# Which engine forms the low parts of seven-product weight forms, and when x's fourth form is made

## The chip, the cores and the metric

The kernel runs on one core of one Trainium2 chip. The metric is the device time of one execution in microseconds (us), the median over several runs. A core has TensorE (PE: matmuls; PEld is its weight load), VectorE (DVE), ScalarE (ACT), GpSimd (POOL) and SyncE (SP), each with an instruction queue of its own that it works off in order, and 16 DMA engines that all queues share. An instruction that has to wait holds up everything behind it in its queue. Here SP issues the loads of weights, and GpSimd issues DMAs that add.

## The reference

Two layers on x of 512 tokens by 1024 features, in float32. Each layer is an FFN, a mixer, a second FFN and a gated input embedding, each followed by a LayerNorm of `ALPHA * x + sublayer(x)`:

```python
def swiglu_ffn(x, w_gu, w_d):
    g, u = jnp.split(x @ w_gu, 2, axis=-1)
    return (jax.nn.silu(g) * u) @ w_d
...
for i in range(DEPTH):
    x = layer_norm(DN_ALPHA * x + 0.5 * swiglu_ffn(x, ffn1_wgu[i], ffn1_wd[i]), ln_g[i, 0], ln_b[i, 0])
    ... mixer: mlstm_mixer in layer 0, gmlp_mixer in layer 1
    x = layer_norm(DN_ALPHA * x + 0.5 * swiglu_ffn(x, ffn2_wgu[i], ffn2_wd[i]), ln_g[i, 2], ln_b[i, 2])
    ... gated embedding
```

The hidden width of the FFN is 2816, which is 22 blocks of 128. There are four FFNs; the change touches nothing else.

## The kernel before, in words

**High and low parts.** TensorE multiplies float32 in a reduced form (`F32R`). So each operand is cut into a high part, ScalarE's rounded copy, and a low part, the operand less its high part, and a product is three matmuls: high by high, x's low by the weight's high, x's high by the weight's low (`mm3`, L351 to L355). The low part is made in one of two ways:

```python
self.nc.vector.tensor_sub(lo[:, s], src[:, s], hi[:, s].bitcast(F32))       # on VectorE: L251, or later L257
...
self.nc.scalar.activation(lo[:, s], src[:, s], AF.Copy, scale=-1.0)         # by DMA: ScalarE, L248,
self.nc.gpsimd.dma_start(lo[:, s], src[:, s], accum_op=OP.add)              # then GpSimd's adding DMA, L249
```

**Chunks.** `ffn` works through the 22 hidden blocks in six chunks of 2, 4, 4, 4, 4 and 4. In chunks 0 to 3 gate and up columns of a block are plain products of x (tile `fps`, L1145 to L1149). In chunks 4 and 5 a pair of blocks (gate g and up u, two raw weight tiles of 1 MB) is made with seven products in place of eight, in the manner of Strassen and Winograd: x is cut into quarters (two halves of the features by two halves of the tokens), the raw weights too, and sums of quarters are multiplied. This document calls the four pairs of an FFN A and B (chunk 4), C and D (chunk 5), and their products A0 to A6 and so on. Each goes into tile `ups`.

**Weight forms.** `up_forms` makes the seven forms of a pair in the raw tiles themselves: 0 (`a11`) and 1 (`a12`) are gate quarters as loaded; 2 (`s2`) is two VectorE instructions (L141, L142) that write over gate quarter 0; 3 (`s1`) is the up sum left there; 4 (`s3`) is two more (L149, L150) that write over gate quarter 1 and over gate quarter 0, that is, over form 2; 5 (`s4`) is what stands in gate quarter 1; 6 (`a22`) is an up quarter. Form 4 can only be made when the parts of forms 1 and 2 are taken (`self.after`). `UP_BY_DMA` lists the forms whose low part is made by DMA; the rest are made on VectorE, and in chunks 4 and 5 (`W.apart`) that subtraction is put off: it is issued at the next `W.lows()`, and the form counts as made from then on (L257, function `done`). A form by DMA counts as made at once, when its DMA is issued.

**Down products.** The down projection of chunk c - 1 runs in chunk c, also with seven products (`Group`, tile `gps`, weights `wquarter`), one after each odd step. Each adds into x's residual on VectorE (L727). Its weight forms always have their low parts on VectorE.

**The order of a step.** In chunks 4 and 5, `up_products` writes out one step s per up product: the product; the residual add of the last down product (L727); on the seventh product the gating (L1064, and a split in chunk 5); the copy of the product's bank out of PSUM (ScalarE, L1045) or an add onto it (VectorE, L1048, L1050); the put-off low parts; on some steps of chunk 4 an entry of `formed.last`; `W.release()`, which hands the product's weight buffer on and so cuts the form four products ahead (ScalarE's high part, L242); Silu; `W.form_ahead(3)`, which makes the sums of the next three forms if they may be made; on odd steps the down product and the cutting of the next form of h (L905, L908). A product r needs bank 0 free for r = 2, 4 and 6, bank 3 for r = 5.

**Loads.** There are three raw buffers. `done` counts down the uses of a raw tile and issues the next load on SP as soon as a tile has none left, that is, after forms 4 and 5 of a gate tile and 3 and 6 of an up tile. On the device the load waits for whoever reads the tile last.

**x's forms.** `UpForms` makes four sums of x's quarters, once per FFN. `steps` is a list of small functions: in chunk 3 two are run per block index i from `FORM_AT` on (L1161), and what is left at the end of that chunk. `last` maps a step of chunk 4 to a function: step 0 the low part of t2 and both parts of t3 (L994 and, over the quarter of x itself, L358 and L359), step 2 the sum `x21` (tile `x_d`, L964), step 3 `t4` (L1002, and copies on ScalarE, L1003), step 4 `t4_low` (L1008, tile `t_f`). Product 2 uses t2, 3 uses t1, 4 uses t3, 6 uses t4.

Of the kernel before, what the change touches and what calls it, by code (L numbers as in the profile page):

```python
# [10 lines left out]
F32 = mybir.dt.float32  # L11
F32R = mybir.dt.float32r
AF = mybir.ActivationFunctionType
# [29 lines left out]
W_BUFS = 4  # L43
EXTRA = 2
PLE_EXTRA = 3
UP_BY_DMA = (1, 2, 4)


class Weights:
# [77 lines left out]
    def up_forms(self, g, u):  # L127
# [34 lines left out]
        self.after.update({s2: (a11,), s3: (a12, s2)})  # L162
        self.by_dma.update(made[r][1] for r in UP_BY_DMA)
        return [("main", js, make) for js, make in made]
# [158 lines left out]
def hybrid_trunk(ctx: ExitStack, tc, x, p, ln_g, ln_b, ffn1_wgu, ffn1_wd, ffn2_wgu, ffn2_wd,  # L323
# [25 lines left out]
    vec, sca, pool = nc.vector, nc.scalar, nc.gpsimd  # L349
# [7 lines left out]
    def split(hi, lo, src):  # L357
        sca.activation(hi, src, AF.Copy)  # L358
        vec.tensor_sub(lo, src, hi.bitcast(F32))  # L359
# [75 lines left out]
    FFN_CHUNKS = [2, 4, 4, 4, 4, 4]  # L435
    LAST = len(FFN_CHUNKS) - 1
    UP_FROM = 4
    FORM_AT = 3
    turn_p = []

    def ffn_weights(wgu, wd, name, ple=False):
# [231 lines left out]
    class Norm:  # L673


        def __init__(self, layer, k, out=None):
            self.out, self.st, self.rs = out, {}, {}
            self.deferred = out is None and k != 2
            self.at = (layer * 4 + k) * KB
            gb = act.tile([P, 2, D], F32, name="gb", tag="gb")  # L680
            self.g_bc, self.b_bc = gb[:, 0], gb[:, 1]
            o = (layer * 4 + k) * D
            sca.dma_start(self.g_bc, row_ap(ln_g, o, D))
            sca.dma_start(self.b_bc, row_ap(ln_b, o, D))
# [51 lines left out]
    def run_affine(n=1):  # L736
        for _ in range(n):
            if affine:
                affine.pop(0)()
# [210 lines left out]
    class UpForms:  # L950


        def __init__(self, pool, late):

            f32 = lambda at, tag: at.tile([P, 4, 256], F32, name="x_" + tag, tag=tag)
            a = [tmp.tile([P, 2, 256], F32, name="x_a", tag="pad", bufs=3) for _ in range(2)]
            b, c = f32(late, "wlo"), f32(pool, "f0")
            both = act.tile([P, 2, 4, 256], F32R, name="t1", tag="gb")
            self.t1, self.t2, self.t4 = [both[:, 0], both[:, 1]], [], []
            self.t3 = self.quarter(0, 1)  # L960
            whole, halves = slice(0, 4), (slice(0, 2), slice(2, 4))

            def joined(dst, k, t, s=whole):
                vec.tensor_add(dst, *(p[:, s].bitcast(F32) for p in self.quarter(k, t)))  # L964

            def f32r(to, at, tag):
                to.append(at.tile([P, 4, 256], F32R, name="t_" + tag, tag=tag))
                return to[-1]

            def x22():  # L970
                for i, s in enumerate(halves):
                    joined(a[i], 1, 1, s)

            def t3():
                for i, s in enumerate(halves):
                    vec.tensor_sub(b[:, s], a[i], b[:, s])

            def t1():
                for i, s in enumerate(halves):
                    vec.tensor_sub(a[i], a[i], c[:, s])  # L980

            def split_t1():
                for i, s in enumerate(halves):
                    split(self.t1[0][:, s], self.t1[1][:, s], a[i])

            self.steps = [
                x22, lambda: joined(b, 0, 1), t3, lambda: joined(c, 0, 0), lambda: vec.tensor_add(c, b, c),
                lambda: sca.activation(f32r(self.t2, late, "whi"), c, AF.Copy), t1, split_t1]

            d = [tmp.tile([P, 2, 256], F32, name="x_d", tag="pad", bufs=3) for _ in range(2)]  # L990

            def t3_t2():
                split(*self.t3, b)
                vec.tensor_sub(f32r(self.t2, late, "wlo"), c, self.t2[0].bitcast(F32))  # L994

            def x21():
                for i, s in enumerate(halves):
                    joined(d[i], 1, 0, s)

            def t4():  # L1000
                for i, s in enumerate(halves):
                    vec.tensor_sub(d[i], d[i], c[:, s])  # L1002
                    sca.activation(f32r(self.t4, pool, "f1")[:, s] if not i else self.t4[0][:, s], d[i], AF.Copy)  # L1003

            def t4_low():
                lo = f32r(self.t4, pool, "f0")
                for i, s in enumerate(halves):
                    vec.tensor_sub(lo[:, s], d[i], self.t4[0][:, s].bitcast(F32))  # L1008

            self.last = {0: t3_t2, 2: x21, 3: t4, 4: t4_low}  # L1010
            self.right = [self.quarter(0, 0), self.quarter(1, 0), self.t2, self.t1, self.t3,
                          self.quarter(1, 1), self.t4]

# [55 lines left out]
    def ffn(layer, k, rows, late, prepare=None):  # L1069
        with stage_pool("forms", 2) as fpool, stage_pool("quarters", Q_BUFS) as qpool, \  # L1070
# [53 lines left out]
            for c, n in enumerate(FFN_CHUNKS):  # L1124
# [13 lines left out]
                for i in range(2 * n if c < UP_FROM else 0):  # L1138
# [20 lines left out]
                    if c == 1 and i < 3:  # L1159
                        run_affine()  # L1160
                    if formed is not None and i >= FORM_AT:  # L1161
                        formed.step()
# [745 lines left out]
```

## Time and profile before

| | us |
|---|---|
| median of 3 runs | 2288.68 |
| lowest and highest | 2285.99, 2288.74 |
| the profiled execution | 2286.79 |
| its span in the profile | 2285.1 |
| mean granted clock of TensorE | 0.985 |

The span is one execution as the hardware profiler saw it. Times in the rows below count from its start. "Busy" is time in which an engine worked; an instruction's row has its start, its duration, engine, line, tiles, and in square brackets how long the engine stood idle before it and what ended that. VectorE's instructions follow each other a little quicker than their durations say (a subtraction of 128 x 1024 lasts 1.22 us, the next begins 1.14 us after it). The chain of waits is followed back from the last instruction, at each step to what released it. The four FFNs' chunks 4 and 5 lie at about 213 to 350, 983 to 1120, 1411 to 1546 and 2053 to 2190 us.

### The profile page before, as it was taken

Reading aid. Unit: us, or ns where it says so; the run is one execution under the profiler, and the core shown is the slowest. Engines: PE = TensorE matmul, PEld = TensorE weight load, DVE = VectorE, ACT = ScalarE, POOL = GpSimd, SP = SyncE. Lnnn points to the kernel's source line nnn. Section 1 sums busy time; section 2 is a strip of 40 time slices with the busy share of each in tenths; the row PEclk is TensorE's granted clock in tenths of the full one; section 3 lists DMA queues with packets and bytes.
Section 4 is the critical chain, followed back from the end, with each engine's and each line's share of the span. In section 5 each row is a group of like instructions: output and inputs, shape, how many; then the busy total and the mean of one; then the engine's idle time right before and its main releaser. Section 6 shows DMA issues by size and latency. Waiting matters only on the chain.

```text
span 2285.1 us, 29387 instructions
## 1 busy us (share of the span) xinstructions
PE 2214.1 (97%) x11669; PEld 1908.1 (84%) x11669; DVE 1711.5 (75%) x2468; ACT 1049.7 (46%) x1476; POOL 145.4 (6%) x183
## 2 busy tenths in 40 slices
PE   9999889999999999989899999889999999998898
PEld 8888888888888888889788888887888888888887
DVE  5668887776776776788786768777788767688887
ACT  4335556464646533355354335545345453345532
POOL 1000000111101000000000000000011100000000
PEclk9999999999999999999999999999999999999999
DMA  6324543466747443335432324543438733344441
GB/s 200 104 87 127 150 118 122 103 152 128 163 111 148 127 141 101 100 95 148 129 124 86 117 78 123 146 127 114 138 75 158 174 102 111 102 120 133 104 142 56
DMA packets 213233, 278.91 MB, mean 122 GB/s; under 512 B 6580, under 2 KB 161332, under 8 KB 213096
## 3 DMA queue, kind: packets, MB, share of 16 engines
q1 hardware_dynamic: 168080, 211.83, 28.8%
q0 software_dynamic: 38400, 50.52, 14.1%
q10 hardware_dynamic: 6616, 14.69, 2.0%
q8 instruction: 92, 1.51, 0.3%
q14 instruction: 45, 0.37, 0.1%
HBM read 224.58 MB, written 2.11 MB: 99 GB/s over the span
## 4 chain that ended last, share of the span: by engine, by line
PE 84%; DVE 9%; ACT 2%; DMA 2%; issue 2%; DVEq 0%; ACTq 0%; POOL 0%; POOLq 0%
PE fps L353 8%; PE fps L355 8%; PE fps L354 8%; PE gps L355 6%; PE gps L353 6%; PE gps L354 6%; DVE wlo L257 3%; PE ups L354 2%; PE ups L353 2%; PE ups L355 2%; PE dps L354 2%; PE dps L353 2%; PE dps L355 2%; DMA wlo<-wraw 2%; PE gups L353 1%
## 5 line engine op out<-in xcount | busy, mean ns | idle before, releaser
L242 ACT ACTIVATE whi<-wraw 128x1024 fp32r<-128x1024 f32 (+1 forms) x388 | 400.5, 1048 | 206.9 <-DVE wraw L142 64.3
L353 PE MATMUL fps<-xh,whi 128*128 128x512 f32 x800 | 311.4, 389 | 0.0
L354 PE MATMUL fps<-xl,whi 128*128 128x512 f32 x800 | 311.3, 389 | 0.0
L355 PE MATMUL fps<-xh,wlo 128*128 128x512 f32 x800 | 311.2, 389 | 0.0
L251 DVE TENSOR_TENSOR wlo<-wraw,whi 128x1024 fp32r<-128x1024 f32 (+1 forms) x210 | 252.4, 1217 | 48.0 <-ACT whi L242 47.2
L353 PE MATMUL gps<-whi,fhi 128*128 128x512 f32 x644 | 251.9, 391 | 0.0
L354 PE MATMUL gps<-wlo,fhi 128*128 128x512 f32 x644 | 251.6, 391 | 0.0
L355 PE MATMUL gps<-whi,flo 128*128 128x512 f32 x644 | 251.3, 390 | 0.0
L242 ACT ACTIVATE whi<-wquarter 128x1024 fp32r<-128x1024 f32 (+1 forms) x140 | 136.0, 971 | 221.5 <-PE gps L355 141.4
L251 DVE TENSOR_TENSOR wlo<-wquarter,whi 128x1024 fp32r<-128x1024 f32 (+1 forms) x92 | 97.7, 1062 | 160.8 <-ACT whi L242 160.8
L249 POOL DMA_DIRECT2D wlo<-wraw x96 | 100.7, 1049 | 1515.9 <-ACT wlo L248 1328.0
L727 DVE TENSOR_TENSOR xt<-xt,gps 128x512 f32<-128x512 f32 x302 | 193.9, 682 | 3.1 <-PE gps L355 2.8
L355 PEld LDWEIGHTS fps<-xh,wlo 128*128 128x128 f32 x800 | 150.1, 188 | 31.2
L353 PEld LDWEIGHTS fps<-xh,whi 128*128 128x128 f32 x800 | 150.2, 188 | 31.1
L354 PEld LDWEIGHTS fps<-xl,whi 128*128 128x128 f32 x800 | 150.2, 188 | 31.1
L353 PE MATMUL ups<-xh,whi 128*128 128x256 f32 x512 | 145.2, 284 | 0.0
L354 PE MATMUL ups<-xl,whi 128*128 128x256 f32 x512 | 145.0, 283 | 0.0
L355 PE MATMUL ups<-xh,wlo 128*128 128x256 f32 x512 | 145.0, 283 | 0.0
L355 PEld LDWEIGHTS gps<-whi,flo 128*128 128x128 f32 x644 | 120.9, 188 | 26.2
L905 ACT ACTIVATE fhi<-h 128x512 fp32r<-128x512 f32 (+1 forms) x140 | 81.0, 579 | 131.6 <-DVE h L1149 47.5
L353 PEld LDWEIGHTS gps<-whi,fhi 128*128 128x128 f32 x644 | 121.2, 188 | 23.9
L354 PEld LDWEIGHTS gps<-wlo,fhi 128*128 128x128 f32 x644 | 121.1, 188 | 23.7
(361 smaller groups left out, 5104.7 us busy)
## 6 DMA issues: line engine op xcount, KB each, us to landing
wraw<-in_ffn_wgu_dram SPq DMA_DIRECT2D x79, 1024.0 KB, 7.1
wlo<-wraw POOLq DMA_DIRECT2D x96, 512.0 KB, 5.2
wquarter<-in_ffn_wd_dram SPq DMA_DIRECT2D x64, 512.0 KB, 3.8
wraw<-in_ml_w_in_dram SPq DMA_DIRECT2D x24, 1024.0 KB, 5.6
wraw<-in_gm_w_in_dram SPq DMA_DIRECT2D x15, 1024.0 KB, 5.5
wraw<-in_ffn_wgu_dram SPq DMA_DIRECT2D x17, 512.0 KB, 5.0
wraw<-in_ffn_wd_dram SPq DMA_DIRECT2D x8, 1024.0 KB, 5.0
wraw<-in_ml_w_out_dram SPq DMA_DIRECT2D x8, 1024.0 KB, 4.9
```

Source lines behind the costliest of these rows:

```text
L242: self.nc.scalar.activation(hi[:, s], src[:, s], AF.Copy)
L249: self.nc.gpsimd.dma_start(lo[:, s], src[:, s], accum_op=OP.add)
L251: self.nc.vector.tensor_sub(lo[:, s], src[:, s], hi[:, s].bitcast(F32))
L257: self.nc.vector.tensor_sub(lo, src, hi.bitcast(F32))
L353: mm(ps, st[0], mv[0], start=start, stop=False, skip_group_check=more)
L354: mm(ps, st[0], mv[1], start=False, stop=False, skip_group_check=more)
L355: mm(ps, st[1], mv[0], start=False, stop=stop, skip_group_check=more)
L727: vec.tensor_add(dst, dst, ps)
L905: sca.activation(hi, src, AF.Copy)
```

## The change

- `UP_BY_DMA` goes from forms 1, 2 and 4 to forms 1, 4, 5 and 6. So form 2's low part is made on VectorE, those of forms 5 and 6 by ScalarE and a DMA.
- `x21` and `t4` go from steps 2 and 3 of chunk 4 to the end of `steps`, and so into chunk 3; `t4_low` goes from step 4 to step 3.
- `FORM_AT` goes from 3 to 2: the steps of chunk 3 begin one block index earlier.
- `t4` takes its tile ahead of the loop, and `x21` and `t4` stand before `t3_t2` in the text; these two change no instruction.

```diff
-UP_BY_DMA = (1, 2, 4)
+UP_BY_DMA = (1, 4, 5, 6)
...
-    FORM_AT = 3
+    FORM_AT = 2
...
+            def x21():
+                for i, s in enumerate(halves):
+                    joined(d[i], 1, 0, s)
+
+            def t4():
+                hi = f32r(self.t4, pool, "f1")
+                for i, s in enumerate(halves):
+                    vec.tensor_sub(d[i], d[i], c[:, s])
+                    sca.activation(hi[:, s], d[i], AF.Copy)
+
             def t3_t2():
                 split(*self.t3, b)
                 vec.tensor_sub(f32r(self.t2, late, "wlo"), c, self.t2[0].bitcast(F32))
-
-            def x21():
-                for i, s in enumerate(halves):
-                    joined(d[i], 1, 0, s)
-
-            def t4():
-                for i, s in enumerate(halves):
-                    vec.tensor_sub(d[i], d[i], c[:, s])
-                    sca.activation(f32r(self.t4, pool, "f1")[:, s] if not i else self.t4[0][:, s], d[i], AF.Copy)
...
-            self.last = {0: t3_t2, 2: x21, 3: t4, 4: t4_low}
+            self.steps += [x21, t4]
+            self.last = {0: t3_t2, 3: t4_low}
```

More of the change, by code (lines that the diff above doesn't have):

```diff
@@ L990, in __init__ @@
             d = [tmp.tile([P, 2, 256], F32, name="x_d", tag="pad", bufs=3) for _ in range(2)]
-            def t3_t2():
-                split(*self.t3, b)
-                vec.tensor_sub(f32r(self.t2, late, "wlo"), c, self.t2[0].bitcast(F32))
             def x21():
@@ L1000, in t4, with t3_t2 @@
             def t4():
+                hi = f32r(self.t4, pool, "f1")
                 for i, s in enumerate(halves):
                     vec.tensor_sub(d[i], d[i], c[:, s])
-                    sca.activation(f32r(self.t4, pool, "f1")[:, s] if not i else self.t4[0][:, s], d[i], AF.Copy)
+                    sca.activation(hi[:, s], d[i], AF.Copy)
+            def t3_t2():
+                split(*self.t3, b)
+                vec.tensor_sub(f32r(self.t2, late, "wlo"), c, self.t2[0].bitcast(F32))
             def t4_low():
```

## The prediction

> **What bounds the kernel now.** I read the page first, then busy time by stage, then what TensorE waits for, and last the timelines of VectorE, ScalarE and the load queue inside one stage. From the page:
>
> ```profile
> PE 2214.1 (97%) x11669; PEld 1908.1 (84%) x11669; DVE 1711.5 (75%) x2468; ACT 1049.7 (46%) x1476; POOL 145.4 (6%) x183
> PE 84%; DVE 9%; ACT 2%; DMA 2%; issue 2%; DVEq 0%; ACTq 0%; POOL 0%; POOLq 0%
> ```
>
> TensorE is busy 97% of 2285.1 us, so its whole idle time is 71 us. The chain that ended last is TensorE for 84% and VectorE for 9%, so in some places VectorE decides. Busy time by stage (columns: stretch, length, then busy us of PE, PEld, DVE, ACT, POOL, then clock, DMA share, GB/s):
>
> ```profile
> 213.00:350.00 137.00, 124.30 (x848) 116.38 (x848) 110.73 (x132) 72.11 (x91) 8.41 (x10) 0.95 0.48 128
> 350.00:983.00 633.00, 630.69 (x3120) 530.92 (x3119) 460.62 (x803) 315.05 (x477) 59.74 (x75) 1.00 0.50 125
> ```
>
> The first row is chunks 4 and 5 of the first FFN, the part made with seven products a pair: 12.7 us of it are idle on TensorE, against 2.3 us in the 633 us behind it. VectorE works 110.7 of 137 us there. What TensorE waits for (line, who releases it: total, times, longest), and VectorE's one long wait:
>
> ```profile
> PE ups L353 <- ACT us L1045: 28.4, 4, 8.1
> PE ups L354 <- DVE t_f L1008: 23.1, 4, 5.8
> PE dps L353 <- DVE xt L727: 4.3, 2, 2.2
> PE dps L353 <- ACT whi L242: 2.4, 2, 1.2
> PE dps L354 <- DVE wlo L257: 1.5, 2, 0.8
> DVE wraw L150 <- DMA wlo<-wraw: 54.5, 12, 5.4
> ```
>
> Each of the four FFNs has two stops. **Stop 1** (23.1 us in all) is product A6, which waits for the low part of x's fourth form, the last thing VectorE does in step 4. **Stop 2** (28.4 us) is product D2, whose bank ScalarE has not yet copied out, because ScalarE stands behind VectorE. VectorE itself stands 54.5 us at L150: that writes over the third form (s2) and must wait until the DMA that makes s2's low part has read it. In the first FFN:
>
> ```profile
> 213.27 0.28 PE L353 MATMUL ups<-xh,whi 128*128 128x256 f32 x1
> 239.08 0.35 PE L353 MATMUL ups<-t_f,whi 128*128 128x256 f32 x1 [0.18 <-DVE us L1050]
> 245.20 0.58 PE L354 MATMUL ups<-t_f,whi 128*128 128x256 f32 x1 [5.77 <-DVE t_f L1008]
> 249.89 0.28 PE L353 MATMUL ups<-xh,whi 128*128 128x256 f32 x1
> 252.76 0.40 PE L353 MATMUL gps<-whi,fhi 128*128 128x512 f32 x1
> 324.72 0.58 PE L353 MATMUL ups<-t_whi,whi 128*128 128x256 f32 x1 [6.75 <-ACT us L1045]
> ```
>
> An up product takes 2.87 us (249.89 to 252.76). A6 begins at 239.08, after six up products and three down products, so a down product takes (239.08 - 213.27 - 17.2) / 3 = 2.9 us; its second matmul, the first that reads the low part, then stands from 239.4 to 245.2. After each stop TensorE also runs slowly. Five microseconds behind both stops of the first and third FFN, and behind the short stops at the end of the second and the first:
>
> ```profile
> 245.20:250.20 5.00, 5.00 (x26) 5.00 (x27) 4.64 (x5) 1.94 (x3) 0.00 (x0) 0.58 0.59 152
> 324.70:329.70 5.00, 4.98 (x27) 4.89 (x28) 5.00 (x7) 5.00 (x7) 0.85 (x1) 0.68 0.34 65
> 1441.50:1446.50 5.00, 4.97 (x23) 4.97 (x24) 4.67 (x5) 1.91 (x2) 0.00 (x0) 0.50 0.58 152
> 1521.70:1526.70 5.00, 5.00 (x25) 5.00 (x26) 5.00 (x7) 4.78 (x6) 0.84 (x1) 0.57 0.34 66
> 1122.20:1127.20 5.00, 4.24 (x11) 3.15 (x12) 5.00 (x5) 4.69 (x5) 0.00 (x0) 0.66 0.30 67
> 356.60:361.60 5.00, 5.00 (x22) 4.16 (x23) 4.17 (x8) 0.00 (x0) 0.57 (x1) 1.00 0.62 235
> ```
>
> Granted clocks of 0.58, 0.68, 0.50 and 0.57 over 5 us lose 2.1, 1.6, 2.5 and 2.15 us: 4.2 us an FFN, 16.7 us for four. So the two stops cost 23.1 + 28.4 + 16.7 = 68.2 us. That is the ceiling of what this change can take away, because it leaves TensorE's instructions as they are.
>
> **The change part by part.** VectorE's rows in the first FFN:
>
> ```profile
> 209.62 1.29 DVE L359 TENSOR_TENSOR t<-x_a,t 128x512 fp32r<-128x512 f32 x2 [1.45 <-ACT t L358]
> 213.47 0.69 DVE L1149 SCALAR_TENSOR_TENSOR h<-sg,fps 128x512 f32<-128x512 f32 x1 [0.76 <-PE fps L355]
> 217.92 1.22 DVE L359 TENSOR_TENSOR xl<-x_wlo,xh 128x1024 fp32r<-128x1024 f32 x1 [0.57 <-ACT xh L358]
> 228.84 1.22 DVE L257 TENSOR_TENSOR wlo<-wraw,whi 128x1024 fp32r<-128x1024 f32 x1
> 229.97 1.22 DVE L257 TENSOR_TENSOR wlo<-wquarter,whi 128x1024 fp32r<-128x1024 f32 x1
> 231.11 1.29 DVE L964 TENSOR_TENSOR x_d<-xh,xl 128x512 f32<-128x512 f32 x2
> 235.85 1.29 DVE L1002 TENSOR_TENSOR x_d<-x_d,x_f 128x512 f32<-128x512 f32 x2
> 240.25 0.69 DVE L908 TENSOR_TENSOR flo<-h,fhi 128x512 fp32r<-128x512 f32 x1 [1.32 <-ACT fhi L905]
> 244.46 1.29 DVE L1008 TENSOR_TENSOR t_f<-x_d,t_f 128x512 fp32r<-128x512 f32 x2
> 255.17 1.23 DVE L150 TENSOR_TENSOR wraw<-wraw 128x1024 f32<-128x1024 f32 x1 [5.30 <-DMA wlo<-wraw]
> 273.56 1.23 DVE L141 TENSOR_TENSOR wraw<-wraw 128x1024 f32<-128x1024 f32 x1 [1.42 <-DMA wraw<-in_ffn_wgu_dram]
> 283.10 1.23 DVE L150 TENSOR_TENSOR wraw<-wraw 128x1024 f32<-128x1024 f32 x1 [2.99 <-DMA wlo<-wraw]
> 317.56 1.23 DVE L150 TENSOR_TENSOR wraw<-wraw 128x1024 f32<-128x1024 f32 x1 [5.32 <-DMA wlo<-wraw]
> 321.28 0.69 DVE L359 TENSOR_TENSOR wquarter<-us,wquarter 128x512 fp32r<-128x512 f32 x1 [0.70 <-ACT wquarter L358]
> 321.89 0.68 DVE L1064 SCALAR_TENSOR_TENSOR us<-us,ups 128x512 f32<-128x512 f32 x1
> ```
>
> and one row each of ScalarE's (a low part's first half) and of the load queue's:
>
> ```profile
> 311.59 1.04 ACT L248 ACTIVATE wlo<-wraw 128x1024 fp32r<-128x1024 f32 x1
> 266.36 3.35 SPq L208 DMA_DIRECT2D wraw<-in_ffn_wgu_dram  x2
> ```
>
> *x's fourth form.* Its sum (231.11) and difference (235.85) leave steps 2 and 3 of chunk 4, 1.20 us of VectorE each, with two copies of 0.6 us on ScalarE; its low part moves from step 4 to step 3. It then stands where 235.85 stood, and the 2.4 us ahead of it are gone or stand in chunk 3: it ends at about 235.4, some 4 us before A6 asks at 239.4. Stop 1 goes. None of these steps issues a DMA.
>
> *Chunk 3 takes them in.* It gets 2.4 us for the fourth form and 1.14 us (228.84 to 229.97 is one low part behind another) for the third form's low part of pair A, 3.5 us in all. Against that stand idle 1.45 us at 209.62 and 0.76 us at 213.47, and the steps begin one block earlier. Queued behind the added work are h (213.47) and t3's low part (217.92). The bounds are 0 and 3.5 us late; walking the queue I come to 1.5 us, since the idle 1.45 us moves to the earlier block while the new low part waits about 1.1 us for its high part. TensorE feels this through A4: its sums end 1.4 us later than now, ScalarE's low half begins at 225.2, and from there the finished DMA takes 6.0 us (311.59 to 317.56, where L150 is let go): 231.1. TensorE is there at 213.3 + 4 x 2.87 + 2 x 2.9 + 0.2 = 230.8. **New stop at A4: 0.3 us.**
>
> *Third form on VectorE.* Four low parts an FFN more on VectorE, four ScalarE halves and DMAs fewer. L150 now reads what VectorE itself wrote before, so its waits (54.5 us in all) have nothing to wait for. The sums are made one step later, since the form counts as made only when its low part has been issued.
>
> *Sixth and seventh form by DMA.* Eight low parts an FFN leave VectorE (8 x 1.14), eight halves of 1.04 us come to ScalarE, which is busy 72 of 137 us, and eight DMAs. They are made four products ahead, 4 x 2.87 + 2 x 2.9 = 17.3 us, and need 1 + 6.0 us: hidden, with 10 us to spare. What isn't hidden is that a raw buffer is given back only when the DMA has read it. On SP the next raw load waits for that, with the loads of the next down quarters queued behind it; who waits in the end is VectorE at L141, and behind it on VectorE the residual adds and the gating. Pair C's second load starts at 266.36 now and L141 goes on at 273.56, 7.2 us later. After the change I get B5's halves on ScalarE at 255.6 to 257.6, the DMA done at 262.5, the load landed at 269.7.
>
> *Sum for VectorE up to pair C's gating.* Now it goes from 217.92 to 322.5, 104.6 us, of which 1.32 + 5.30 + 1.42 + 2.99 + 5.32 + 0.70 = 17.05 us are idle: 87.5 us of work. After: 87.5 - 2.4 (fourth form) - 6 x 1.14 (A5 to C6) + 2 x 1.14 (B2, C2) - 2.4 (D4's two sums come behind) = 78.1 us. It starts at 219.4, waits 2.5 us for TensorE at B4 (it is ahead there), 5.8 us for the load (at L141 from 263.9 to 269.7) and 0.7 us for ScalarE: 306.5. Then a split, a down form's low part and D2's: D2 ready at 309.8. TensorE reached D2 at 324.72 - 6.75 = 318.0; without stop 1 and its slow stretch, at 318.0 - 5.95 - 2.1 = 309.9 (5.95 is 0.18 + 5.77). **Stop 2 falls to about 0.2 us.** D4's sums end at 313.4, its high and low halves 2.0 us later, its DMA at 320.2; TensorE comes at 309.9 + 2 x 2.87 + 2.9 + 0.2 = 318.7. **New stop at D4: 1.5 us.**
>
> *Clock behind short stops.* The bounds are 0 (356.60, after a stop of 2.2 us) and 1.7 us (1122.20, clock 0.66 after stops of 1.2 and 0.8 us); nothing places D4 nearer to one, so 0.85. The Trainium skill, "TensorE: Matmul & The Clock Gate", Part 1, has the clock halved only after an idle window of about 3.4 us; by that the term would be 0 and the sum 3.4 us better. The row at 1122.20 shows otherwise, so 0.85 stays.
>
> Left over per FFN: 0.3 + 0.2 + 1.5 + 0.85 = 2.85 us, and 0.2 us as my estimate for accumulates that overlap (A4's and A5's are issued 2 us apart): 3.05 us; four times, 12.2 us. **Gain 68.2 - 12.2 = 56.0 us.** The profiled execution took 2286.8 us (1.7 us around its span) and would take 2230.8; the median of before is 2288.7, 1.9 us above it, so I forecast 2232.7 us.
>
> **The rivals.** *All stops go* (VectorE 2 us quicker than I walk it): 68.2 us off, 2220.5 us. For it: VectorE is ahead of TensorE at B4. Against: D4's DMA starts behind VectorE's tail.
>
> *The raw load becomes the bound.* Pair C's load lands 5 us later than I have it, from accumulates that overlap with loads (each load now starts right behind one). VectorE has no gap left behind L141, so the 5 us are passed on whole to D2, which then stops long enough for 2.1 us of slow clock (245.20) in place of 0.85. Left per FFN: 3.05 + 5 + 1.25 = 9.3 us, gain 31.0 us, 2257.7 us. Against: now the wait at 273.56 is only 1.42 us. The Trainium skill, "DMA: Bandwidth & Descriptors", section on issuing engines not being separate queues, speaks for this: GpSimd's transfers run on the same 16 engines as SP's and interleave with them.
>
> *Stop 1 comes back at the start of chunk 4*: all 3.5 us of the work put into chunk 3 reach TensorE, at the third product, with 2.5 us of slow clock (1441.50): 3.05 + 6.0 us left per FFN, gain 32 us, 2256.7 us. Against: the idle rows at 209.62 and 213.47.
>
> *Slower: the sixth and seventh forms' DMAs land too late.* TensorE then waits at 32 products. They have 17.3 us and need 7; beyond 17.3 us each microsecond costs 32, and at 19.1 the gain of 56 is gone. At 19.2 us the time is 2288.7 - 56.0 + 32 x 1.9 = 2293.5 us. That needs an accumulate three times as slow as the 6.0 us shown.
>
> *Nothing*: another wait holds VectorE at L150 as long as the DMA did. Its other inputs were there before, by the rows; 2288.7 us.
>
> **How the numbers follow.** Forecast 0.56, its own range 2222 to 2247 (left over 0.5 to 6.5 us an FFN); all stops go 0.15; raw load 0.14; start of chunk 4 0.08; slower 0.04; nothing 0.03. The range takes in all the faster cases, 2217 to 2260. Faster by over 0.2% (4.6 us, about what a measurement of this kernel can tell from no change) 0.93, within it 0.03, slower 0.04.
>
> **What would show it.** Right: no wait of TensorE for t_f L1008; none of VectorE at L150 for a DMA; VectorE's wait at L141 for a load grows to 4 to 8 us in chunk 4 of each FFN; TensorE's waits in these stages are below 4 us an FFN, at D2 or D4, and for a low part by DMA. Wrong: a wait at the third product of chunk 4 for t2's low part; a wait at D2 of 5 us or more behind a late L141; waits at fifth, sixth or seventh forms throughout.

## The result, and the profile after

| | before | after |
|---|---|---|
| median, 4 runs each (us) | 2288.08 | 2247.98 |
| lowest and highest | 2285.99, 2288.74 | 2246.35, 2251.26 |
| the profiled execution | 2286.79 | 2251.26 |
| its span | 2285.1 | 2249.5 |

The change makes the kernel faster: the ratio is 0.9831, with a 95% interval of 0.9818 to 0.9845, and the medians are 40.1 us apart. The profiled execution of after is the slowest of its four, and stands 35.5 us below that of before. The forecast was 2232.7 us. One execution of x_form_only (4451 us) and one of after_again (2564 us), two kernels below, took far longer than the others of the same kernel, and the ratios leave them out.

From the page of after, the engines' busy times:

```profile
PE 2207.3 (98%) x11669; PEld 1896.6 (84%) x11669; DVE 1693.8 (75%) x2452; ACT 1059.5 (47%) x1492; POOL 159.0 (7%) x199
```

The work moved as the diff says: VectorE has 16 instructions fewer, ScalarE 16 more, and GpSimd issues 16 more adding DMAs (112 in place of 96). What TensorE waits for in after (total, times, longest), and then VectorE's wait for a raw load:

```profile
PE ups L353 <- ACT us L1047: 12.2, 12, 2.5
PE dps L353 <- DVE xt L727: 7.0, 3, 3.5
PE ups L354 <- DVE t_wlo L1004: 5.1, 4, 1.3
...
PE ups L355 <- DMA wlo<-wraw: 2.2, 3, 1.1
...
PE ups L355 <- DVE wlo L257: 0.4, 2, 0.2
```

```profile
DVE wraw L141 <- DMA wraw<-in_ffn_wgu_dram: 25.0, 5, 6.8
```

(Lines from `UpForms` on have moved: L1004 is t2's low part, L1009 `t4_low`, L1047 the copy of a bank, L1061 Silu, L1066 the gating.) The 23.1 us for t4's low part are gone, and so is VectorE's wait of 54.5 us at L150. In their place stand small stops: 12.2 us for copies of banks, at three places in an FFN (A4, C4 and D4), 5.1 us for t2's low part, and a longer one at `dps`, behind chunk 5.

Where did the time come from? I cut out, in each FFN, the stretch from the first up product of chunk 4 to the first `dps` product behind chunk 5. The first of the four and the sum of all four (length, then busy us of PE, PEld, DVE, ACT, POOL), before:

```profile
213.27:348.81 135.54, 122.84 (x842) 115.19 (x840) 110.35 (x132) 71.17 (x90) 8.41 (x10) 0.95 0.48 126
sum 551.26, PE 496.70 PEld 465.08 DVE 440.80 ACT 285.83 POOL 33.94; mean PE 124.18 PEld 116.27 DVE 110.20 ACT 71.46 POOL 8.48
```

and after:

```profile
212.74:339.38 126.64, 122.11 (x842) 113.47 (x841) 105.22 (x128) 75.55 (x96) 12.64 (x15) 0.99 0.60 146
sum 510.42, PE 488.09 PEld 452.36 DVE 420.02 ACT 302.86 POOL 50.91; mean PE 122.02 PEld 113.09 DVE 105.01 ACT 75.71 POOL 12.73
```

The four stretches are 40.8 us shorter: 32.2 us less idle time of TensorE (551.26 - 496.70 against 510.42 - 488.09) and 8.6 us less busy time for the same matmuls, with a mean clock of 0.99 in place of 0.95 in the first stretch. The rest of the kernel, span less these stretches, went from 1733.8 to 1739.1 us: 5.2 us were lost where the forecast saw nothing.

The first FFN in after, in order of time (timelines of VectorE, ScalarE, GpSimd, the load queue and TensorE):

```profile
221.53 1.23 DVE L1004 TENSOR_TENSOR t_wlo<-x_f,t_whi 128x1024 fp32r<-128x1024 f32 x1
222.81 0.38 PE L354 MATMUL ups<-t_wlo,whi 128*128 128x256 f32 x1 [1.29 <-DVE t_wlo L1004]
235.25 1.29 DVE L1009 TENSOR_TENSOR t_f<-x_d,t_f 128x512 fp32r<-128x512 f32 x2
252.25 1.23 DVE L150 TENSOR_TENSOR wraw<-wraw 128x1024 f32<-128x1024 f32 x1
259.23 0.83 POOL L249 DMA_DIRECT2D wlo<-wraw  x1 [2.52 <-ACT wlo L248]
266.62 0.37 SPq L208 DMA_DIRECT2D wraw<-in_ffn_wgu_dram  x1
273.74 1.23 DVE L141 TENSOR_TENSOR wraw<-wraw 128x1024 f32<-128x1024 f32 x1 [6.84 <-DMA wraw<-in_ffn_wgu_dram]
291.04 0.68 DVE L1050 TENSOR_TENSOR us<-us,ups 128x512 f32<-128x512 f32 x1
291.75 0.63 ACT L1061 ACTIVATE us<-us 128x512 f32<-128x512 f32 x1 [3.09 <-DVE us L1050]
293.76 0.57 ACT L1047 ACTIVATE us<-ups 128x512 f32<-128x512 f32 x1
294.38 0.39 PE L353 MATMUL ups<-xh,whi 128*128 128x256 f32 x1 [2.37 <-ACT us L1047]
313.70 1.22 DVE L257 TENSOR_TENSOR wlo<-wraw,whi 128x1024 fp32r<-128x1024 f32 x1
315.84 0.28 PE L353 MATMUL ups<-t_whi,whi 128*128 128x256 f32 x1
```

At 252.25 VectorE passes L150 without a wait. At 259.23 the adding DMA of B5 (sixth form) is issued; the load of pair C's second tile into the tile that it reads is let go at 266.62, and VectorE stands 6.84 us for it. From there to 291.04 VectorE is never idle for 0.1 us, and it doesn't catch up: its add at 291.04 is late, Silu at 291.75 stands for it on ScalarE, the copy of bank 0 stands behind Silu, and C4 behind the copy. D2 itself (315.84) no longer waits.

The 5.2 us outside are at the end of the first and third FFN (3.8 and 2.0 us; the other parts are 0.5 us shorter together). After the first FFN (timelines of GpSimd, the load queue, ScalarE and TensorE), with the five microseconds behind the stop, and the row of the load at 332.22 in the list of DMAs, whose last number is us from issue to landing:

```profile
327.11 0.85 POOL L249 DMA_DIRECT2D wlo<-wraw  x1 [2.06 <-ACT wlo L248]
332.22 0.37 SPq L208 DMA_DIRECT2D wraw<-in_ml_w_in_dram  x1
342.39 1.06 ACT L242 ACTIVATE whi<-wraw 128x1024 fp32r<-128x1024 f32 x1 [0.76 <-DMA wraw<-in_ml_w_in_dram]
345.49 1.06 ACT L242 ACTIVATE whi<-wraw 128x1024 fp32r<-128x1024 f32 x1 [1.09 <-DMA wraw<-in_ml_w_in_dram]
348.46 0.80 PE L353 MATMUL dps<-whi,wquarter 128*128 128x512 f32 x1 [3.48 <-DVE xt L727]
```

```profile
348.40:353.40 5.00, 4.94 (x12) 3.88 (x13) 4.17 (x9) 0.00 (x0) 0.57 (x1) 0.50 0.40 153
```

```profile
wraw<-in_ml_w_in_dram SPq DMA_DIRECT2D x1, 1024.0 KB, 10.2
```

The mixer's first weights go into the raw tile that D6's adding DMA (327.11) reads until 332.1, so their load begins at 332.22. It then lands only after 10.2 us, at 342.4, among other loads that were also held up. ScalarE stands for it, and at 345.49 for the next one; VectorE's low parts wait for ScalarE, and the last residual adds stand behind those. The same stop was 2.16 us in before, with a clock of 1.00 behind it (the prediction's row at 356.60); now it is 3.48 us with 0.50, which loses 2.5 us more. 1.3 + 2.5 = 3.8 us is what the stretch from there to the second FFN's chunk 4 grew by (634.8 to 638.6 us).

### The profile page after: what moved, and what is told of

It reads as the page before. It is cut to its first block, busy times and chain, and to the rows that moved or that the text cites. A ratio compares the mean times of both kernels' runs of the same rounds, so it can differ in the third digit from the quotient of the medians.

```text
span 2249.5 us, 29438 instructions
## 1 busy us (share of the span) xinstructions
PE 2207.3 (98%) x11669; PEld 1896.6 (84%) x11669; DVE 1693.8 (75%) x2452; ACT 1059.5 (47%) x1492; POOL 159.0 (7%) x199
## 5 line engine op out<-in xcount | busy, mean ns | idle before, releaser
L251 DVE TENSOR_TENSOR wlo<-wraw,whi 128x1024 fp32r<-128x1024 f32 (+1 forms) x214 | 257.0, 1216 | 52.5 <-ACT whi L242 51.9
L249 POOL DMA_DIRECT2D wlo<-wraw x112 | 114.2, 1020 | 1500.5 <-ACT wlo L248 1309.6
L355 PEld LDWEIGHTS fps<-xh,wlo 128*128 128x128 f32 x800 | 150.2, 188 | 31.3
L353 PE MATMUL ups<-xh,whi 128*128 128x256 f32 x512 | 147.6, 288 | 12.2 <-ACT us L1047 12.2
```

The costliest lines, as they stand in the source:

```text
L353: mm(ps, st[0], mv[0], start=start, stop=False, skip_group_check=more)
L355: mm(ps, st[1], mv[0], start=False, stop=stop, skip_group_check=more)
```

## The experiments

Two accounts stood at the start. One: the stops add up, so each part of the change takes away its own stop and its own time. The other: everything passes through one VectorE queue, a stop removed early is given back at D2 as long as VectorE is late there, and only what shortens VectorE's way counts.

**The two parts alone.** In dma_part_only the kernel before has only this edit, and x's form stays:

```diff
-UP_BY_DMA = (1, 2, 4)
+UP_BY_DMA = (1, 4, 5, 6)
```

> Only the list of forms by DMA is changed (second, fifth, sixth, seventh); x's fourth form stays in chunk 4. Theory A (each stop has a cause of its own and both parts of the change are needed): stop 1 stays, TensorE waits some 20 to 24 us for t_f in all; VectorE's waits at L150 for a DMA are gone, stop 2 is below 8 us in all; time about 2262 us, 26 us less than before. Theory B (one VectorE queue decides, whatever TensorE waited for earlier): VectorE ends pair C's gating hardly later than in the changed kernel, the rest of the stops shrinks by what stop 1 takes, time 2250 to 2256 us.

2254.87 us, ratio 0.9863 [0.9847, 0.9878]. TensorE's waits for t4's low part and for banks:

```profile
PE ups L354 <- DVE t_f L1008: 17.8, 4, 4.5
PE ups L353 <- ACT us L1045: 4.8, 4, 1.8
```

In x_form_only the changed kernel goes back on that edit alone:

```diff
-UP_BY_DMA = (1, 4, 5, 6)
+UP_BY_DMA = (1, 2, 4)
```

> Only x's fourth form is moved to chunk 3; the forms by DMA are those of before. Theory A, additive (the parts are worth the same alone): stop 1 is gone with its slow clock, 23 + 9 us, time about 2257 us. Theory B, one VectorE queue: TensorE comes to D2 8 us earlier and waits there longer; only the 2.4 us of VectorE's work that left chunk 4 are won per FFN, stop 2 grows from 7 to about 12 us each, time about 2278 us.

2272.04 us, 0.9935 [0.9918, 0.9951]. TensorE's waits for banks and for a down product's low part, and VectorE's at L150:

```profile
PE ups L353 <- ACT us L1047: 26.7, 8, 6.8
PE gps L354 <- DVE wlo L257: 9.5, 4, 2.4
DVE wraw L150 <- DMA wlo<-wraw: 53.3, 12, 5.4
```

The second account is the nearer one, but it had the place wrong. Moving x's form takes stop 1 away (23.1 us and its slow clock), yet gains 14.0 us where the first account expected some 32 and the second 11: VectorE still stands 53.3 us at L150. The stops at D2 did not grow to 12 us each, they stayed at 6.2 to 6.8. What came back came earlier in the queue: in the first FFN VectorE goes on from L150 at 251.21, makes a down form's low part behind it, and the down product at 256.62 waits 2.4 us for that, as one does in every FFN. The DMA part alone gains 31.2 us and shortens even stop 1. Alone the two gain 45.2 us, together 40.1. The stretches show both sides: the part by DMA makes them 34.8 us shorter (551.26 to 516.44), but the rest of the kernel 5.9 us longer; x's form makes them 13.8 us shorter and leaves the rest alone.

**Which of the forms.** Both of these are the changed kernel but for one line, dma_2_5 and then dma_2_5_7 (`UP_BY_DMA` counts from 0, so its 5 and 6 are the sixth and the seventh form):

```diff
-UP_BY_DMA = (1, 4, 5, 6)
+UP_BY_DMA = (1, 4)
```

```diff
-UP_BY_DMA = (1, 4, 5, 6)
+UP_BY_DMA = (1, 4, 6)
```

> The changed kernel with only the second and fifth form by DMA: the sixth and seventh go back to VectorE, the third stays there. Theory C (late raw loads): VectorE's wait at L141 for a load in chunk 4 falls from 7 to below 3 us, which pays for most of the 6.8 us an FFN of low parts that VectorE gets back up to pair C's gating; 2248 to 2256 us. Theory D (VectorE's work decides): the 6.8 us come back whole, some 2270 to 2275 us.

> The changed kernel with the sixth form's low part back on VectorE: second, fifth and seventh by DMA. The gate tile of pair B is then free as soon as VectorE has made that low part, and VectorE stands idle there (3.2 us ahead of L908 in the changed kernel). Theory C (late raw loads): pair C's second load starts some 5 us earlier, the wait at L141 falls from 6.8 to about 2 us, the stops at C4 and D4 (2.4 and 0.5 us in the first FFN) go, about 2238 us. Theory D (VectorE's work decides): 2.3 us an FFN more on VectorE, 2250 to 2257 us.

dma_2_5: 2240.75 us, 0.9801 [0.9784, 0.9817], faster than the changed kernel though VectorE makes eight low parts an FFN more, and 7 us below the range of theory C. dma_2_5_7: 2244.82 us, 0.9819 [0.9804, 0.9834], which neither theory gave. In dma_2_5, VectorE's wait at L141, and after the first FFN the mixer's first load (start, and in the list of DMAs) and the stop at `dps`:

```profile
DVE wraw L141 <- DMA wraw<-in_ffn_wgu_dram: 7.4, 4, 2.0
```

```profile
326.64 0.37 SPq L208 DMA_DIRECT2D wraw<-in_ml_w_in_dram  x1
345.44 0.50 PE L353 MATMUL dps<-whi,wquarter 128*128 128x512 f32 x1 [2.16 <-DVE xt L727]
```

```profile
wraw<-in_ml_w_in_dram SPq DMA_DIRECT2D x1, 1024.0 KB, 5.4
```

Without the sixth and seventh form's DMAs the gate tile comes back early. At the end of the FFN the mixer's first load starts 5.6 us earlier and lands in 5.4 us, and the `dps` stop is 2.16 us again: theory C had not counted this gain. In dma_2_5_7 the load starts as early as hoped, but not alone (timelines of the load queue, GpSimd and VectorE):

```profile
261.30 0.37 SPq L208 DMA_DIRECT2D wraw<-in_ffn_wgu_dram  x1
261.73 0.85 POOL L249 DMA_DIRECT2D wlo<-wraw  x1 [4.48 <-ACT wlo L248]
272.19 1.23 DVE L141 TENSOR_TENSOR wraw<-wraw 128x1024 f32<-128x1024 f32 x1 [5.69 <-DMA wraw<-in_ffn_wgu_dram]
```

It takes 10.9 us from its start to VectorE, where the load at 266.62 above takes 7.1 us. So whether this load starts early or late, pair C's second tile is there at about 272 to 274.

**x's steps one index earlier still.** The index that `FORM_AT` is compared with counts gate and up columns, 0 to 7 in chunk 3, so one index is half a hidden block. TensorE waited 1.29 us for t2's low part in every FFN, and the steps of chunk 3 can begin at index 1. On one chip I ran the changed kernel again (after_again), the changed kernel with this edit (after_at1), and this edit with `UP_BY_DMA = (1, 4)` (dma_2_5_at1) and `(1,)` (dma_2_at1):

```diff
-    FORM_AT = 2
+    FORM_AT = 1
```

> The changed kernel once more, on the chip of the next three, for the comparison: 39 to 41 us less than before on the same chip, about 2246 us.

> The changed kernel with x's steps begun at block index 1 of chunk 3 instead of 2 (one index earlier). Theory E (the last block indexes of chunk 3 are too full, so t2's low part comes late): the wait of TensorE at the third product of chunk 4 for t2's low part, 5.1 us in all, goes, and VectorE starts chunk 4 about 1.3 us earlier; 6 to 8 us less than the changed kernel. Rival (VectorE's lag behind the late raw load decides the rest): only the stop itself moves on to C4 and D4, within 2 us of the changed kernel.

> Second and fifth form by DMA, the rest on VectorE, and x's steps from block index 1. Theory E: the third product's wait (5.1 us) goes; A4's, B4's and D4's waits for the fifth form's DMA (9.1 us in 12) shrink by the 1.3 us that VectorE is earlier, to below 4 us; about 2232 us. Rival (VectorE's total decides with seven low parts more on it): 2240 us, as without the earlier start.

> As dma_2_5_at1, but the fifth form's low part on VectorE too: only the second by DMA. Theory F (the fifth form's 6 us by DMA behind its sums is what is left): no wait of TensorE for a DMA, at most 2 us better than dma_2_5_at1, because 1.14 us a pair come onto VectorE; about 2231 us. Theory D (VectorE's work decides by now): 4 x 4 x 1.14 = 18 us of work more shows at C4 and D2 as waits for ScalarE's copy, 2236 to 2250 us.

The results were 2247.44 us, 0.9832 [0.9819, 0.9846], for after_again; 2235.61, 0.9784 [0.9771, 0.9797], for after_at1; 2229.86, 0.9757 [0.9744, 0.9771], for dma_2_5_at1; and 2235.28, 0.9776 [0.9762, 0.979], for dma_2_at1. In after_at1, t2's low part begins at 219.23, 2.3 us earlier than in after, and the stop is gone. The gain of 11.8 us is more than the 5.1 us of that stop and more than was expected; in the profiled executions the stretches are 10.1 us shorter than after_again's (492.32 against 502.42). Of these, 6.9 us are idle time of TensorE: 5.1 us at A2, 0.8 us at A4, the rest at C4 and D4, although VectorE's work in the stretches falls by 2.6 us an FFN (from 419.95 to 409.47 us). The other 3.2 us are busy time for the same matmuls (484.41 against 481.19) at a clock of 1.00 in both; the section on the prediction says what I take that to be. In dma_2_5_at1 TensorE's waits for low parts by DMA were 6.5 us, where less had been expected. In dma_2_at1 no product waits for a DMA, but VectorE is late again:

```profile
PE ups L353 <- ACT us L1047: 8.4, 8, 1.8
```

So VectorE has room for the sixth and seventh form's low parts, and, as it looks, not for the fifth's as well: the medians are 5.4 us apart, but the intervals of the two ratios overlap.

**The sixth or the seventh alone.** With `FORM_AT = 1` as above, dma_2_5_6_at1 has the first of these lines, dma_2_5_7_at1 the second, and the third is the best kernel again:

```diff
+UP_BY_DMA = (1, 4, 5)
...
+UP_BY_DMA = (1, 4, 6)
...
+UP_BY_DMA = (1, 4)
```

> Second, fifth and sixth form by DMA, x's steps from block index 1. Theory G (the sixth form by DMA gives the gate tile back late, so pair C's second load lands late): the wait at L141 is back at 5 us or more in chunk 4, and most of the 5 to 6 us between the variants with four and with two forms by DMA is here: about 0.978 of before. Theory H (the seventh form's DMA shares the engines with the loads): 0.976, as with two forms.

> Second, fifth and seventh form by DMA, x's steps from block index 1. Theory G: the gate tile is free early, but the load that then runs beside the seventh form's DMA landed 10.9 us after its start in the run without the early steps, so TensorE waits for the seventh form's DMA: 0.977 to 0.978 of before. If only the sixth form's hold on the gate tile mattered: 0.976.

> Second and fifth form by DMA, x's steps from block index 1, once more on the chip of the other two: 0.9757 of before, within 0.0015.

2241.91 us, 0.98 [0.9786, 0.9813], with the sixth; 2235.09, 0.9771 [0.9757, 0.9784], with the seventh; 2231.09, 0.9752 [0.9739, 0.9766], with neither. In the first FFN with the sixth (GpSimd, load queue, VectorE):

```profile
257.49 0.85 POOL L249 DMA_DIRECT2D wlo<-wraw  x1 [2.53 <-ACT wlo L248]
264.19 0.37 SPq L208 DMA_DIRECT2D wraw<-in_ffn_wgu_dram  x1
270.98 1.23 DVE L141 TENSOR_TENSOR wraw<-wraw 128x1024 f32<-128x1024 f32 x1 [5.64 <-DMA wraw<-in_ffn_wgu_dram]
```

and with the seventh:

```profile
258.42 0.37 SPq L208 DMA_DIRECT2D wraw<-in_ffn_wgu_dram  x1
258.83 0.85 POOL L249 DMA_DIRECT2D wlo<-wraw  x1 [4.48 <-ACT wlo L248]
271.82 1.23 DVE L141 TENSOR_TENSOR wraw<-wraw 128x1024 f32<-128x1024 f32 x1 [8.23 <-DMA wraw<-in_ffn_wgu_dram]
```

and with neither:

```profile
260.08 0.37 SPq L208 DMA_DIRECT2D wraw<-in_ffn_wgu_dram  x1
267.75 1.23 DVE L141 TENSOR_TENSOR wraw<-wraw 128x1024 f32<-128x1024 f32 x1 [2.29 <-DMA wraw<-in_ffn_wgu_dram]
```

The sixth form's DMA holds the tile (its load goes 6.7 us after the adding DMA was issued, and then takes 6.8 us); the seventh's does not hold that tile, but the load takes 13.4 us. With neither it takes 7.7 us. Theory G comes nearer in both (it had 0.978, and 0.977 to 0.978).

In these traces the load is slow while the packets of adding DMAs move, not as soon as one is issued. With the seventh form, the queues of the adding DMAs (q0) and of the loads (q1) in the window 264 to 270 (packets, MB, share of the 16 engines' time; packets can overlap):

```profile
q0 software_dynamic: 271, 1.00, 84.2%
q1 hardware_dynamic: 404, 0.40, 22.7%
```

In dma_2_5_7 the shares are 78.7% and 25.5% from 266 to 272. With the sixth form an adding DMA is issued at 264.23, 0.04 us behind the load, but q0 has 2.5% of the engines up to 270, and VectorE has the tile at 270.98. In the other three FFNs the load takes 7.8 to 10.6 us with the seventh form and 5.5 to 6.6 us with the sixth.

All the kernels side by side; forms are counted from 1, "stretches" is the sum row of each, "rest" its span less that, both of its profiled execution. Each ratio above is against runs of before on the same chip, whose medians were 2286.03, 2286.16 and 2287.64 us.

| kernel | forms by DMA | `FORM_AT` | median | stretches | rest |
|---|---|---|---|---|---|
| before | 2, 3, 5 | 3 | 2288.08 | 551.3 | 1733.8 |
| x_form_only | 2, 3, 5 | 2 | 2272.04 | 537.4 | 1733.0 |
| dma_part_only | 2, 5, 6, 7 | 3 | 2254.87 | 516.4 | 1739.8 |
| after | 2, 5, 6, 7 | 2 | 2247.98 | 510.4 | 1739.1 |
| after_again | 2, 5, 6, 7 | 2 | 2247.44 | 502.4 | 1740.8 |
| dma_2_5_7 | 2, 5, 7 | 2 | 2244.82 | 508.0 | 1734.7 |
| dma_2_5 | 2, 5 | 2 | 2240.75 | 503.8 | 1734.8 |
| dma_2_5_6_at1 | 2, 5, 6 | 1 | 2241.91 | 504.2 | 1735.3 |
| after_at1 | 2, 5, 6, 7 | 1 | 2235.61 | 492.3 | 1741.0 |
| dma_2_at1 | 2 | 1 | 2235.28 | 498.8 | 1733.1 |
| dma_2_5_7_at1 | 2, 5, 7 | 1 | 2235.09 | 498.7 | 1734.2 |
| dma_2_5_at1 | 2, 5 | 1 | 2229.86 | 490.7 | 1735.9 |
| dma_2_5_at1_again | 2, 5 | 1 | 2231.09 | 492.9 | 1735.2 |

The last column falls in two groups. It is 1739.1 to 1741.0 us in the four profiles with both the sixth and the seventh form by DMA, and 1733.0 to 1735.9 in the nine others. With `FORM_AT = 1` that is the whole price of these two: the stretches with them (492.3) and without (490.7, 492.9) are the same. Either alone leaves the last column as it was (1735.3, 1734.2) and lengthens the stretches instead (504.2, 498.7). As I read it, the load is late all the same, and VectorE then has the other form's low parts to make behind it; no run separates this.

## Why the prediction was right, and where it was not

**Right.** The kernel became faster, by 40.1 us of the 56.0 forecast. The median lies in the wide range (2217 to 2260), 1 us outside the forecast's own (2222 to 2247), and nearer to the rivals at 2257.7 and 2256.7 than to 2232.7. Stop 1 went, for the reason given: `t4_low` begins at 235.25 and ends at 236.5 (forecast 235.4). The waits at L150 went, and D2 waits 0.2 us in two FFNs and not at all in the others (forecast 0.2). VectorE's wait at L141 grew as the prediction said it would: 6.84, 6.77, 4.57 and 6.61 us in the four FFNs (forecast 5.8). No product waits at sixth or seventh forms for long: 2.2 us in all for low parts by DMA.

**Right by chance.** A4 waits 0.20 us (forecast 0.3) and D4 0.5 to 1.8 us (forecast 1.5), but not for the fifth form's DMA, as forecast: both wait for ScalarE's copy of a bank (L1047). The sign "below 4 us an FFN, at D2 or D4, and for a low part by DMA" failed: TensorE waited 4.5, 6.0, 3.7 and 5.7 us in the four FFNs, 12.2 us of it for such copies, nearly all at C4 and D4.

**The step that failed.** "Left over per FFN ... 3.05 us; four times, 12.2 us" was too small; the ceiling was not. In the profiled execution there are left 12.2 + 5.1 + 2.2 + 0.4 = 19.9 us of stops in the stretches, at least 7.4 us of longer busy time (488.09 us against 480.64 in dma_2_5_at1, for the same matmuls), and 5.2 us in the rest of the kernel: 32.6 us. 68.2 - 32.6 = 35.6 us, and the span fell by 35.6 us. For after_again the same sum is 15.4 + 3.8 + 6.9 = 26.1 us left, 42.1 us gained, and its span of 2243.2 us is 41.9 us below that of before. The median lies between. Four terms were mis-sized or left something out:

- *The rest of the kernel, forecast 0, measured 5.2 to 6.9 us.* "Who waits in the end is VectorE at L141" stopped short: what D5 and D6 hold are the tiles of the next loads, the mixer's among them. I followed a late raw tile within the stage and not past its end. The column above, and the `dps` stop with and without these DMAs, show it; it takes both forms.
- *Chunk 3 takes the steps in, 1.5 us late and felt at A4.* t2's low part began at 221.53, and in before at 219.18: 2.35 us late, and TensorE felt it already at A2, 1.29 us in every FFN, 5.1 us in all. The prediction listed this wait as one that would show it wrong, and so it does for this step, at about a fifth of the rival's price (6.0 us an FFN).
- *The load of pair C, "landed 269.7".* I had B5's DMA done at 262.5; it was issued at 259.23 instead of 257.6 and, 3.4 us behind B4's, took 7.3 us; the load began at 266.62, and VectorE went on at 273.74, 4 us later than walked. VectorE's own work was forecast well: from 220.28 to the end of pair C's gating at 311.8 it worked 78.7 us (forecast 78.1), but was idle 12.8 us instead of 9.0 and began 0.9 us later. VectorE was ready for D2's low part at 314.9 instead of 309.8. But this lag was not passed on to D2: it stopped TensorE at C4 (2.37, 1.62, 0.54 and 2.49 us), through the add, Silu and copy above. With that stop, the slow clock behind it and the stop at A2, D2 came 5.9 us later than walked (315.84 against 309.9) in the first FFN and found its weights ready. The rival "the raw load becomes the bound" named the cause and about its size, and the wrong product.
- *Clock behind short stops, 0.85 us an FFN.* In the stretches of the profiled execution the clock fell behind two stops only, 2.37 us at C4 of the first FFN and 1.77 us at D4 of the second, each to 0.66 over 5 us: 1.7 us each, 3.4 us in all, which is 0.85 an FFN by chance. In after_again it stayed at 1.00 in all four stretches. What was left out is that a short stop costs more than its idle row at full clock too. At A2 in after the matmul ahead of the stop began at 221.24 and the next one at 222.81, where matmuls like these follow each other at 0.12 us: 1.45 us were lost, and 0.1 us more behind it, for an idle row of 1.29 us. I take the other 4.0 of the 7.4 us, and the 3.8 us of after_again, to be this; they were not added up stop by stop. The Trainium skill, "TensorE: Matmul & The Clock Gate", Part 1, has the clock halve after about 3.4 us without work. The row at 348.40 agrees (3.48 us, clock 0.50); the stop at C4 of the first FFN does not, as the last section shows.

Two executions of the changed kernel differ in the C4 stops (7.0 us in all, against 1.7 in after_again) with the same instructions. Which transfers meet differs from run to run; what decides it I did not find.

**The better version.** Second and fifth form by DMA, the other low parts on VectorE, and x's steps from index 1: 2229.9 and 2231.1 us on two chips, 0.9757 and 0.9752. The useful parts of the change are the third form on VectorE, which frees L150 (x_form_only and dma_2_5 differ in nothing else, and by 31.3 us), and the earlier x form. The sixth and seventh form by DMA relieve VectorE of work that it has room for.

A fourth raw buffer, which might take the tile's return off the path, was not tried.

## What to carry to other kernels

When work moves from an engine to a DMA that reads a buffer in place, ask when that buffer is given back and to whom, and follow it past the end of the stage: here the loss was at the next stage's first load. A DMA's duration read alone is a lower bound where the change makes several run together. And when a stop early in an in-order queue is removed, expect the time back only as far as the later stops in that queue are removed too.

## What the runs showed that I had not expected

A load's time depends on what moves beside it. From its start to VectorE the 1 MB load of pair C took 7.1 us in after, 10.9 us in dma_2_5_7 and 13.4 us in dma_2_5_7_at1. An adding DMA was issued 0.3 to 0.4 us behind it in all three, so that alone does not decide; where the time was long, the load was not through when adding DMAs began to move, as the shares of the queues above show. Why it was not through in these kernels I did not find. The adding DMA slows down as well. In the list of DMAs (last number: us from issue to landing), the one at 312.93 in before, alone, and B5's at 259.23 in after:

```profile
wlo<-wraw POOLq DMA_DIRECT2D x1, 512.0 KB, 4.5
```

```profile
wlo<-wraw POOLq DMA_DIRECT2D x1, 512.0 KB, 7.3
```

The Trainium skill, "DMA: Bandwidth & Descriptors", section on issuing engines not being separate queues, says that transfers issued by ScalarE, SP and GpSimd run on the same 16 engines and interleave. These rows agree and add the price here: up to six microseconds on a load of seven, and three on an adding DMA of 4.5 (five at 261.73 in dma_2_5_7, which took 9.9 us).

TensorE's clock after a stop does not follow from the length of the stop. Five microseconds behind the stop of 2.37 us at C4 in after, behind the stop of 2.49 us at C4 of its fourth FFN, and behind the stop of 2.16 us at 345.44 in dma_2_5:

```profile
294.40:299.40 5.00, 5.00 (x29) 5.00 (x30) 4.97 (x6) 4.16 (x5) 0.85 (x1) 0.66 0.80 238
2109.80:2114.80 5.00, 4.96 (x41) 4.97 (x42) 4.97 (x6) 4.17 (x5) 0.86 (x1) 1.00 0.79 237
```

```profile
345.40:350.40 5.00, 4.96 (x15) 3.95 (x16) 4.17 (x8) 0.00 (x0) 0.57 (x1) 0.66 0.63 239
```

Behind a stop of the same 2.16 us at the same place in before the clock was 1.00. The stop of 1.77 us at D4 has 0.66 behind it too. So in these runs a stop of about two microseconds is worth up to 1.7 us of slow clock more, and which of them pays is not in the length.
